# Layer 0 of a two-layer decoder: attention outputs and five output weights split once, stored as two parts, and loaded by GpSimd's queue

## Chip, cores and metric

The kernel runs on one core of one Trainium2 chip. The metric is the device time of one execution in microseconds; the time of a kernel is the median of several runs. The engines are PE (matrix products), DVE and ACT (elementwise work), POOL (GpSimd) and SP, which does nothing here but issue transfers. PE's granted clock was 0.999 of full speed in the profiled execution of the kernel before, so the clock plays no part below.

## The reference, cut to what matters

Two layers over a sequence of 1024 positions and 1024 features, all in float32. Layer 0 is differential attention with 8 head pairs, layer 1 forgetting attention; after each come a residual sum with layer norm, a gated feed-forward block with a short convolution, and another layer norm. The change touches layer 0's attention alone:

```python
q, k, v = jnp.split(x @ w_qkv, 3, axis=-1)        # rotary on q and k
p = masked_softmax(s * scale, causal_mask(...))   # two score maps per head pair
a = p[:, :, 0] - lam * p[:, :, 1]
o = rms_norm(jnp.einsum('bhqk,bhkd->bqhd', a, v), subln_g) * (1.0 - lambda_init)
y = o @ w_o                                       # the output projection
h = layer_norm(alpha * h + y, ln1_g, ln1_b)
```

In the kernel the output of pair p is one tile of 128 features by 1024 positions, and the output projection is a sum over the 8 pairs: `y = sum over p of o_p^T @ w_o[p]`, with `w_o[p]` a slab of 128 x 1024.

## The kernel before

**Two parts for each operand.** A float32 product is made of three products of a reduced format: an operand x is split into `h`, the rounded value, and `l = x - h`, and PE adds up `h·h + h·l + l·h` (`mm3`, lines 104 to 110). A split (`split`, lines 93 and 95) is one copy on ACT, which writes `h`, and one subtraction on DVE, which reads x and `h` and writes `l`. Every operand of every projection passes through it once.

**Layer 0, pair by pair.** While the scores, softmax and values of pair p run, PE's spare places are filled with the steps of a second job, one product with a whole slab column block at a time: for p < 7 the projections q, k and v of pair p + 1 (48 steps), for p = 7 the output projection's first part (`out_first`, 64 steps). `pulse` counts these steps, and `after(n, f)` calls f when n more steps have been issued. The instructions thus stand in one written order; a planner of the framework then lays the order of each engine, with a time model of its own: it starts, in the written order's priority, what its model has ready, and gives a tile its place in memory when an earlier tile's last reader is done. On the chip each engine and each issuing queue then works strictly in the order laid. `high_priority` moves a few instructions forward.

**The way of an output.** The values of a pair are made in two groups of four query blocks. When a group is done, `diff_values` copies the result from PE's memory into the pair's tile `of` (line 624), squares it, lets PE sum the squares over features (lines 639 and 640), and scales it by the norm (lines 642 to 647, the last instruction being that of line 647 on DVE). There is one buffer for `of`. After the second group `Values.finish` stores the whole tile, 512 KB, to `od[p]` in memory (line 1625). Since the values lag behind, pair p's store falls in pair p + 1's stretch, and the next user of the buffer is pair p + 1's first copy of line 624. For the output projection `fetch_o` (line 866) loads `od[k]` again and `load_o` splits it into four tiles of 128 x 512, taken from the same 16 + 16 places (`xh`, `xl`) that hold the layer's input while the projections run.

**The output weights.** `ahead(i)` loads slab i raw into one of two `wst` buffers, which the softmax uses too, and `ready(i)` splits it into `wh` and `wl` (three buffers each). Slabs 24 to 31 are the eight of `w_o`. Slab 27 goes into four half tiles (`ready_halves`).

**Queues.** SP issues nearly all transfers: loads, stores, and per pair some 50 small ones for the rotation of q and k and for laying their parts into place. POOL casts one operand of each score product (`qz`, line 548), with two buffers for each of the two heads, and issues a few transfers at the very beginning.

**The beginning.** `first_pair_rotary` runs q and k of pair 0 for both halves of the sequence, rotates them through transfers, runs v, and then the loop over pairs begins. The pool `probT` (tiles `pt`, three buffers) is not used before the first values; the tiles `q1` (seven) are not used before pair 1's projections are done.

Of the kernel before, what the change touches and what calls it, by code (L numbers as in the profile page):

```python
# [9 lines left out]
F32 = mybir.dt.float32  # L10
F32R = mybir.dt.float32r
# [8 lines left out]
P = 128  # L20
# [3 lines left out]
NP = 8  # L24
# [31 lines left out]
W_V, FRAC = 1, 0  # L56
TURN0 = 9
TT1 = 3


class Trunk:
# [319 lines left out]
    def first_pair_rotary(self, t):  # L381


        dst = [self.tmp() for s in range(3)]
        self.xh, self.xl = {}, {}
        pos = self.rope_angles()
        self.nc.scalar.preload_act_table_set("trig_and_small")
        self.warm()
        self.first_loads(pos)
        self.consts()  # L390
        r = {}
        for c in range(2):
            ps = [self.mbank() for _ in range(2)]
            for _ in zip(*[self.dense_steps(ps[s], *self.w[s], c, FILL * (c + s == 0)) for s in range(2)]):
                pass
            if c:
                self.turn(dst, r, 0)
            for s in range(2):
                self.result(0, s, c, ps[s], dst[s], t)
            if c == 0:  # L400
                self.exp_table()
            self.gather(dst, r, c, self.nc.gpsimd)
            if c:
                self.halves(dst, t, 0)
        self.lam()
        for c in range(2):
            self.ready(3) if c else self.ahead(3)
            ps = self.mbank()
            self.dense(ps, *self.w[2], c)
            self.result(0, 2, c, ps, dst[2], t)  # L410
            if c == 0:
                self.turn(dst, r, 1)
                self.halves(dst, t, 1)
            self.after(2 + 2 * c, self.turn_v, 0, c, dst[2], *t[5:7], True)
        self.ahead(4)

    def first_pair(self, l, t):

# [328 lines left out]
    def attention(self, l):  # L747
# [1 line left out]


        nc = self.nc
        self.od = self.dr.tile([NP, P, 1024], F32, name=f"od{l}")
        tiles = lambda p: [self.qtile((p + l) % 2) for _ in range(7)] + (
            [self.lp.tile([P, 1024], F32R, tag="lg", name=self.nm("kl"))] if l else [])
        self.slabs = [self.i[f"w{l}"][s * NP + p] for p in range(NP) for s in range(3)]
# [11 lines left out]
        for p in range(NP):  # L767
# [21 lines left out]
            for job in jobs:  # L789
                live, values = self.tick(live, values, job)  # L790
                w = job[0] + 1 + W_C - (W_V * self.coming(values) if l == 0 else 0)
# [66 lines left out]
    def accumulate(self, acc, ps, alpha):  # L858
        if alpha is None:
            self.nc.vector.tensor_tensor(acc, ps, acc, op=ALU.add)  # L860
        else:
            self.nc.vector.scalar_tensor_tensor(acc, acc, alpha, ps, op0=ALU.mult, op1=ALU.add)

    def fetch_o(self, l, k):
        t = self.lp.tile([P, 1024], F32, tag="lg", name=self.nm("og")) if l == 0 and k < 2 else self.tmp()
        self.nc.sync.dma_start(t, self.od[k])
        self.og[k] = t

    def load_o(self, k, src=None, cs=(0, 1)):
# [28 lines left out]
    def out_ahead(self, l, c):  # L898

        if c == 0:  # L900
            self.oh, self.ol, self.og = {}, {}, {}
            self.fetch_o(l, 0)
            self.after(8, self.load_o, 0, None, (0,))
        else:
            self.ahead(25)
            self.after(3, self.load_o, 0, None, (1,))
            self.after(4, self.fetch_o, l, 1)
            self.after(6, self.ready, 25)
            self.after(8, self.load_o, 1)
# [30 lines left out]
                del self.w[24 + k]  # L940
        self.ready(29)

    def ready_halves(self, i):

        st, self.w[i] = self.stage.pop(i), ([], [])
        for n in range(2):
            for t, which in zip(self.w[i], ("xh", "xl")):
                t.append(self.xtile(which))
            self.split(self.w[i][0][n], self.w[i][1][n], st[:, n * 512:n * 512 + 512])

    def out_first(self):


        self.ahead(26)
        for tt, n in enumerate((0, 0, 0, 0, 0, 16, 22, 28)):
            if n:
                self.after(n, self.acc_tile, tt)
            else:
                self.acc_tile(tt)
        for k, n in ((2, 2), (3, 5), (4, 36), (5, 42), (6, 56)):  # L960
            self.after(n, self.fetch_o, 0, k)
            self.after(n + 4, self.load_o, k)
        self.after(5, self.ready, 26)
        self.after(5, self.ahead, 27)
        self.after(10, self.ready_halves, 27)
        parts = [(tt, (0, 1)) for tt in range(TT1)] + [(tt, (0, 1, 2, 3)) for tt in range(TT1, 8)] + \
            [(tt, (2, 3)) for tt in range(TT1)]
        for i, (tt, ks) in enumerate(parts):
            if i == 8:
                del self.w[24], self.w[25]  # L970
                self.ready(28)
                self.ahead(29)
                self.after(5, self.ready, 29)
                self.after(5, self.ahead, 30)
            elif i == 7:
                self.ahead(28)
            for n in range(2):
                ps = self.mbank()
                for k in ks:
                    self.out_mm(ps, k, tt, n, ks[0], ks[-1])  # L980
                    yield
                self.after(1, self.accumulate, tt, n, ps, ALPHA if ks[0] == 0 else 1.0)
        del self.w[26], self.w[27]
# [575 lines left out]
class Values:  # L1559
# [61 lines left out]
    def finish(self):  # L1621
        if self.end is not None and next(self.end, True):
            self.over = True
            if self.last and self.p < NP - 1:
                self.k.nc.sync.dma_start(self.k.od[self.p], self.k.ofs.pop(self.p))


class Ffn:
# [176 lines left out]
```

## Time and profile before

| | |
|---|---|
| median of 3 runs | 2410.02 us (2407.67 to 2410.25) |
| profiled execution | 2409.52 us, of which 2407.7 us span from first to last instruction |
| PE busy | 2386.8 us, 99% of the span |
| DVE, ACT, POOL busy | 1916.2 us (80%), 1271.1 us (53%), 198.0 us (8%) |
| transferred | 312.25 MB, 130 GB/s on average |
| pair 0's first scores | at 49.6 us |
| the projection of pair 7 ends, the output projection begins | about 418 us |

A line of the profile names the source line, the engine, the operation, then output and inputs by the names of the tiles in the program (`m<-xh,wh`), the shape, and the count; then the busy time, the mean of one in nanoseconds, and the idle time of the engine just before, with what ended it. In a list by time the first two numbers are start and length, and square brackets give the idle time before. An engine with a small q (`SPq`) stands for its issuing queue. `m` and `s` are PE's result memory: four and two buffers.

### The profile page before, as it was taken

How to read it: one execution, taken by the hardware profiler on the slowest of the kernel's cores; microseconds unless marked ns; L12 is line 12 of the kernel's file. 1: busy time of each engine (PE TensorE's matmuls, PEld its weight loads, DVE VectorE, ACT ScalarE, POOL GpSimd, SP SyncE). 2: the span in 40 equal slices, each digit the busy share in tenths (PEclk: the TensorE clock that was granted, in tenths of full speed). 3: DMA queues.
4: the chain of work that ended last, by engine and by line, in shares of the span. 5: the costliest groups of instructions: out<-in, count | busy, mean ns of one | idle time of the engine just before them, and what ended most of it. 6: DMA issues, size and time to landing. Idle time of an engine off the chain costs nothing.

```text
span 2407.7 us, 33873 instructions
## 1 busy us (share of the span) xinstructions
PE 2386.8 (99%) x11691; PEld 1985.8 (82%) x11691; DVE 1916.2 (80%) x3748; ACT 1271.1 (53%) x2405; POOL 198.0 (8%) x396
## 2 busy tenths in 40 slices
PE   9999999999999999999999999999999999999998
PEld 7888887778888888888878888888888888888887
DVE  5888888889987876777767777778899887777768
ACT  4656666556544445444545555555465444445434
POOL 2111111010000110100100000000010001110000
PEclk9999999999999999999999999999999999999999
DMA  6223333521433557876332222224224335559662
GB/s 185 67 78 96 89 86 103 189 95 62 171 119 119 123 134 204 261 227 212 112 82 68 66 67 67 66 95 141 92 79 142 122 118 132 132 142 316 194 232 103
DMA packets 140331, 312.25 MB, mean 130 GB/s; under 512 B 20816, under 2 KB 27984, under 8 KB 140160
## 3 DMA queue, kind: packets, MB, share of 16 engines
q1 hardware_dynamic: 128960, 289.05, 36.9%
q0 software_dynamic: 10912, 20.98, 5.3%
q8 instruction: 92, 1.51, 0.3%
q14 instruction: 79, 0.65, 0.1%
q10 hardware_dynamic: 288, 0.07, 0.0%
HBM read 194.21 MB, written 82.25 MB: 115 GB/s over the span
## 4 chain that ended last, share of the span: by engine, by line
PE 85%; DVE 7%; DMA 3%; ACT 3%; issue 2%; SPq 1%; DVEq 0%; ACTq 0%
PE m L104 19%; PE m L110 19%; PE m L109 19%; PE s L104 5%; PE s L110 5%; PE s L109 5%; PE m L1587 4%; PE s L556 2%; PE s L557 2%; PE m L1614 2%; PE m L1613 1%; DVE xl L95 1%; DVE wo L95 1%; DVE s L564 1%; DMA wb<-in_wd 0%
## 5 line engine op out<-in xcount | busy, mean ns | idle before, releaser
L104 PE MATMUL m<-xh,wh 128*128 128x512 f32 x768 | 314.7, 410 | 1.3 <-DVE pt L95 0.7
L110 PE MATMUL m<-xh,wl 128*128 128x512 f32 x768 | 302.6, 394 | 0.0
L109 PE MATMUL m<-xl,wh 128*128 128x512 f32 x768 | 301.6, 393 | 0.0
L104 PE MATMUL m<-xh,wo 128*128 128x512 f32 x656 | 255.7, 390 | 0.0
L109 PE MATMUL m<-xl,wo 128*128 128x512 f32 x656 | 255.6, 390 | 0.0
L110 PE MATMUL m<-xh,wo 128*128 128x512 f32 x656 | 255.3, 389 | 0.0
L564 DVE CUSTOM_DVE_ANT_0 s<-s,mask 128x384 f32<-128x384 f32 (+7 forms) x256 | 194.2, 760 | 28.0 <-PE s L557 27.2
L93 ACT ACTIVATE wo<-wg 128x512 fp32r<-128x512 f32 (+1 forms) x168 | 102.2, 610 | 169.2 <-PE m L110 141.8
L93 ACT ACTIVATE pt<-m 128x512 fp32r<-128x512 f32 (+3 forms) x285 | 131.1, 490 | 102.5 <-PE m L1587 97.3
L95 DVE TENSOR_TENSOR pt<-m,pt 128x512 fp32r<-128x512 f32 (+3 forms) x285 | 152.7, 557 | 32.6 <-ACT pt L93 30.7
L110 PEld LDWEIGHTS m<-xh,wl 128*128 128x128 f32 x768 | 144.2, 188 | 31.6 <-DVE wl L95 0.7
L104 PEld LDWEIGHTS m<-xh,wh 128*128 128x128 f32 x768 | 144.6, 188 | 27.6 <-DVE pt L95 3.8
L109 PEld LDWEIGHTS m<-xl,wh 128*128 128x128 f32 x768 | 145.0, 189 | 22.8
L548 POOL CAST qz<-q 64x128 fp32r<-64x128 f32 x256 | 94.1, 369 | 819.8 <-PE s L557 726.2
L93 ACT ACTIVATE wo<-t 128x512 fp32r<-128x512 f32 x132 | 83.4, 632 | 127.0 <-PE m L110 81.4
L110 PEld LDWEIGHTS m<-xh,wo 128*128 128x128 f32 x656 | 123.1, 188 | 25.8
L104 PEld LDWEIGHTS m<-xh,wo 128*128 128x128 f32 x656 | 123.3, 188 | 24.7 <-ACT p L1280 0.2
L109 PEld LDWEIGHTS m<-xl,wo 128*128 128x128 f32 x656 | 123.3, 188 | 24.3
L95 DVE TENSOR_TENSOR wo<-wg,wo 128x512 fp32r<-128x512 f32 (+1 forms) x168 | 110.5, 659 | 33.0 <-ACT wo L93 32.3
L556 PE MATMUL s<-q,q 128*128 128x512 f32 (+4 forms) x384 | 133.7, 350 | 1.5 <-ACT wst L602 1.3
L95 DVE TENSOR_TENSOR wo<-t,wo 128x512 fp32r<-128x512 f32 x132 | 90.7, 688 | 49.1 <-ACT wo L93 48.8
L104 PE MATMUL m<-q,wo 128*128 128x512 f32 x328 | 128.6, 392 | 0.0
(386 smaller groups left out, 6328.3 us busy)
## 6 DMA issues: line engine op xcount, KB each, us to landing
wb<-in_wd SPq DMA_DIRECT2D x142, 256.0 KB, 5.4
wst<-in_w SPq DMA_DIRECT2D x46, 512.0 KB, 4.6
t<-in_wi SPq DMA_DIRECT2D x44, 512.0 KB, 5.3
ha<-ad SPq DMA_DIRECT2D x86, 256.0 KB, 4.8
wg<-in_wi SPq DMA_DIRECT2D x42, 512.0 KB, 4.3
ad<-t SPq DMA_DIRECT2D x40, 512.0 KB, 4.1
ha<-sd SPq DMA_DIRECT2D x66, 256.0 KB, 4.3
q<-q SPq DMA_DIRECT2D x128, 128.0 KB, 2.2
```

Source lines behind the costliest of these rows:

```text
L93: self.high = nc.scalar.activation(hi, src, AF.Copy, scale=1.0 if scale is None else scale)
L95: self.low = nc.vector.tensor_tensor(lo, src, hi.bitcast(F32), op=ALU.subtract)
L104: last = mm(out, wh, xh, start=start, stop=False)
L109: mm(out, wh, xl, start=False, stop=False)
L110: mm(out, wl, xh, start=False, stop=stop)
L548: nc.gpsimd.tensor_copy(qz[r:r + 64, :], q[r:r + 64, qt * P:qt * P + P])
L556: nc.tensor.matmul(sb[:, ks], q[:, qt * P:qt * P + P], kd[:, ks], start=True, stop=False)
L557: nc.tensor.matmul(sb[:, ks], qz[:m], kl[:m, ks], start=False, stop=True)
L564: self.nc.vector.tensor_tensor_reduce(sb[:, :ln], sb[:, :ln], self.mask[:, 1024 - ln:], 1.0, BIG, ALU.add, ALU.min, mn)
L1587: nc.tensor.transpose(tb[:, w:w + P], self.pts[q - self.q0][:, kt * P:kt * P + P], k.ident)
L1613: mm(o, self.v[0][:, vs], h, start=first, stop=False)
L1614: mm(o, self.v[0][:, vs], l, start=False, stop=last)
```

## The change

Layer 0 alone changes. The new lines:

- Two steps (`D_PK`) after a group's norm has been written out, `park` splits that half of `of`: `h` goes into a half tile of pool `bcast`, `l` is written over the half of `of` itself. Three steps (`D_PS`) later SP stores both, 256 KB each, to `od[0][p]` and `od[1][p]`. The single store of the whole tile is gone in layer 0.
- At the beginning `park_loads` loads slabs 25 to 29 into `pt` tiles (three, then two), and `park_weights` splits them, `h` into `q1` tiles and `l` in place. `h` is stored to `wd[0]` by ACT's queue, `l` to `wd[1]` by POOL's queue. `lam` and the loads of slabs 3 and 4 are written further ahead.
- In the output projection nothing of pairs 0 to 6 nor of slabs 25 to 29 is split any more. `get_half` loads the two parts of half an output (two transfers of 256 KB), `get_weight` those of a slab (two of 512 KB, or four of 256 KB for slab 27), all on POOL's queue. Slabs 24, 30 and 31 and the output of pair 7 are split as before.
- Three of the residual tiles (`acc_tile`) are loaded 1, 5 and 9 steps into `out_first`, not at its start.

```diff
+D_PK, D_PS, PK0 = 2, 3, 25
...
             self.gather(dst, r, c, self.nc.gpsimd)
+            if c == 0:
+                self.lam()
+                self.ahead(3)
+                self.ahead(4)
+                st = self.park_loads(25, 26, 27)
             if c:
                 self.halves(dst, t, 0)
-        self.lam()
+        self.wd = [self.dr.tile([5, P, 1024], F32, name=f"wd{j}") for j in range(2)]
+        self.park_weights(*st)
         for c in range(2):
-            self.ready(3) if c else self.ahead(3)
+            if c:
+                self.ready(3)
...
                 self.halves(dst, t, 1)
+                self.park_weights(*self.park_loads(28, 29))
             self.after(2 + 2 * c, self.turn_v, 0, c, dst[2], *t[5:7], True)
-        self.ahead(4)
...
+    def park(self, k, of, c):
+        cs = slice(c * 512, c * 512 + 512)
+        h = self.lp.tile([P, 1024], F32R, tag="lg", name=self.nm("ph"))[:, :512]
+        l = of[:, cs].bitcast(F32R)
+        self.split(h, l, of[:, cs])
+        for d, t in zip(self.od, (h, l)):
+            self.after(D_PS, self.nc.sync.dma_start, d[k][:, cs], t.bitcast(F32))
+
+    def park_loads(self, *which):
+        st = []
+        for i in which:
+            st.append((i, self.tt.tile([P, 1024], F32, tag="pt", name=self.nm("wo"))))
+            self.nc.sync.dma_start(st[-1][1], self.slabs[i])
+        return st
+
+    def park_weights(self, *st):
+        for i, t in st:
+            h, l = self.spare(F32R), t.bitcast(F32R)
+            self.split(h, l, t)
+            self.nc.scalar.dma_start(self.wd[0][i - PK0], h.bitcast(F32))
+            self.nc.gpsimd.dma_start(self.wd[1][i - PK0], l.bitcast(F32))
+
+    def get(self, dst, src):
+        for t, d in zip(dst, src):
+            self.nc.gpsimd.dma_start(t.bitcast(F32), d)
+
+    def get_o(self, n, *ks):
+        for i, (k, c) in enumerate((k, c) for k in ks for c in range(2)):
+            self.after(n + 2 * i, self.get_half, k, c)
+
+    def get_half(self, k, c):
+        self.oh[k, c], self.ol[k, c] = self.xtile("xh"), self.xtile("xl")
+        self.get((self.oh[k, c], self.ol[k, c]), [d[k][:, c * 512:c * 512 + 512] for d in self.od])
...
         if c == 0:
             self.oh, self.ol, self.og = {}, {}, {}
+        if l == 0:
+            if c == 0:
+                self.get_o(3, 0, 1)
+            else:
+                self.after(2, self.get_weight, 25)
+                self.get_o(4, 2)
+        elif c == 0:
             self.fetch_o(l, 0)
...
-        self.ahead(26)
-        for tt, n in enumerate((0, 0, 0, 0, 0, 16, 22, 28)):
+        self.get_weight(26)
+        for tt, n in enumerate((0, 0, 1, 5, 9, 16, 22, 28)):
...
-        for k, n in ((2, 2), (3, 5), (4, 36), (5, 42), (6, 56)):
-            self.after(n, self.fetch_o, 0, k)
-            self.after(n + 4, self.load_o, k)
-        self.after(5, self.ready, 26)
-        self.after(5, self.ahead, 27)
-        self.after(10, self.ready_halves, 27)
+        self.get_o(2, 3)
+        self.after(3, self.get_weight, 27, 0)
+        self.after(5, self.get_weight, 27, 1)
+        self.get_o(34, 4, 5)
+        self.get_o(52, 6)
...
             if i == 8:
                 del self.w[24], self.w[25]
-                self.ready(28)
-                self.ahead(29)
-                self.after(5, self.ready, 29)
+                self.get_weight(28)
+                self.after(5, self.get_weight, 29)
                 self.after(5, self.ahead, 30)
-            elif i == 7:
-                self.ahead(28)
...
     def finish(self):
         if self.end is not None and next(self.end, True):
             self.over = True
+            if self.l == 0 and self.p < NP - 1:
+                self.k.after(D_PK, self.k.park, self.p, self.k.ofs[self.p], self.q0 // 4)
             if self.last and self.p < NP - 1:
-                self.k.nc.sync.dma_start(self.k.od[self.p], self.k.ofs.pop(self.p))
+                of = self.k.ofs.pop(self.p)
+                if self.l:
+                    self.k.nc.sync.dma_start(self.k.od[0][self.p], of)
```

More of the change, by code (lines that the diff above doesn't have):

```diff
@@ L751, in attention @@
         nc = self.nc
-        self.od = self.dr.tile([NP, P, 1024], F32, name=f"od{l}")
+        self.od = [self.dr.tile([NP, P, 1024], F32, name=f"od{l}{j}") for j in range(2 - l)]
         tiles = lambda p: [self.qtile((p + l) % 2) for _ in range(7)] + (
@@ L862, in accumulate, with get_weight @@
             self.nc.vector.scalar_tensor_tensor(acc, acc, alpha, ps, op0=ALU.mult, op1=ALU.add)
+    def park(self, k, of, c):
[26 more added lines that the diff above has]
+        self.get((self.oh[k, c], self.ol[k, c]), [d[k][:, c * 512:c * 512 + 512] for d in self.od])
+    def get_weight(self, i, n=None):
+        src = [d[i - PK0] for d in self.wd]
+        if n is None:
+            self.w[i] = [self.wp.tile([P, 1024], F32R, tag=t, name=self.nm(t)) for t in ("wh", "wl")]
+            return self.get(self.w[i], src)
+        w = self.w.setdefault(i, ([], []))
+        for t, which in zip(w, ("xh", "xl")):
+            t.append(self.xtile(which))
+        self.get([t[n] for t in w], [d[:, n * 512:n * 512 + 512] for d in src])
     def fetch_o(self, l, k):
-        t = self.lp.tile([P, 1024], F32, tag="lg", name=self.nm("og")) if l == 0 and k < 2 else self.tmp()
-        self.nc.sync.dma_start(t, self.od[k])
+        t = self.tmp()
+        self.nc.sync.dma_start(t, self.od[0][k])
         self.og[k] = t
@@ L941, in out_early @@
         self.ready(29)
[L943 to L949, printed above, removed]
     def out_first(self):
-        self.ahead(26)
-        for tt, n in enumerate((0, 0, 0, 0, 0, 16, 22, 28)):
+        self.get_weight(26)
+        for tt, n in enumerate((0, 0, 1, 5, 9, 16, 22, 28)):
             if n:
```

## The prediction, written before the change was run

> **What bounds the kernel now.** I read the first page for the share of each engine, then the engines' busy time by stretches, then the waits of PE, then the single stalls in order of time.
>
> ```profile
> span 2407.7 us, 33873 instructions
> PE 2386.8 (99%) x11691; PEld 1985.8 (82%) x11691; DVE 1916.2 (80%) x3748; ACT 1271.1 (53%) x2405; POOL 198.0 (8%) x396
> ```
>
> PE is the bound nearly everywhere: 2407.7 - 2386.8 = 20.9 us of the span are idle on it. The change touches no matmul, so all that it can give back lies in those 20.9 us, and only in those of layer 0's attention, which ends near 530 us. By stretches (columns: window and its length, then busy us and count on PE, PEld, DVE, ACT, POOL, then clock, DMA share, GB/s):
>
> ```profile
> 8.00:66.00 58.00, 57.62 (x265) 47.30 (x263) 35.48 (x94) 28.71 (x59) 14.41 (x32) 1.00 0.55 166
> 344.00:398.00 54.00, 53.51 (x272) 44.31 (x271) 44.11 (x106) 33.11 (x71) 5.09 (x16) 1.00 0.29 82
> 410.00:443.00 33.00, 29.18 (x141) 22.32 (x140) 28.95 (x63) 21.44 (x44) 2.56 (x8) 1.00 0.67 214
> ```
>
> The opening (8 to 66 us) and one pair's stretch (344 to 398) leave PE idle for 0.4 to 0.5 us. The change of work from pair 7's projection to the output projection (410 to 443) leaves 33.00 - 29.18 = 3.8 us, with DVE busy for 28.95 of 33. The stalls there and a little later, each with its length and what ended it:
>
> ```profile
> 413.29 0.66 PE L524 MATMUL m<-ident,t 128*128 128x128 f32 x4 [0.89 <-ACT t L479]
> 420.35 0.50 PE L104 MATMUL m<-wh,xh 128*128 128x512 f32 x1 [0.25 <-ACT xh L93]
> 425.44 0.66 PE L1587 MATMUL m<-ident,p 128*128 128x128 f32 x4 [1.81 <-DVE acc L889]
> 440.82 0.50 PE L104 MATMUL m<-xh,xh 128*128 128x512 f32 x1 [0.82 <-ACT xh L93]
> 487.49 0.50 PE L104 MATMUL m<-wh,xh 128*128 128x512 f32 x1 [0.81 <-DVE acc L889]
> ```
>
> Two more follow when the values of pair 7 and the norm are done; the waits of PE from 410 to 530 name them (total us, times, longest):
>
> ```profile
> PE m L104 <- ACT pt L93: 0.7, 1, 0.7
> PE m L1050 <- DVE acc L1732: 0.3, 1, 0.3
> ```
>
> Together 0.89 + 0.25 + 1.81 + 0.82 + 0.81 + 0.7 + 0.3 = 5.6 us. That is the most this change can win.
>
> **Part 1, what leaves the output projection.** From 404 to 490 us ACT and DVE split the fetched outputs (tiles og and t) and the weights (wst):
>
> ```profile
> L93 ACT ACTIVATE xh<-t 128x512 fp32r<-128x512 f32 x10 | 5.8, 623 | 2.8 <-DMA t<-od 2.7
> L93 ACT ACTIVATE wh<-wst 128x1024 fp32r<-128x1024 f32 x5 | 5.3, 1062 | 6.1 <-DMA wst<-in_wo 4.5 <-PE m L110 1.6
> L95 DVE TENSOR_TENSOR xl<-t,xh 128x512 fp32r<-128x512 f32 x10 | 6.6, 686 | 1.2 <-ACT xh L93 1.2
> L95 DVE TENSOR_TENSOR wl<-wst,wh 128x1024 fp32r<-128x1024 f32 x5 | 6.1, 1220 | 1.4 <-ACT wh L93 1.4
> L95 DVE TENSOR_TENSOR xl<-og,xh 128x512 fp32r<-128x512 f32 x4 | 2.7, 706 | 0.0
> ```
>
> Of the five wide weight splits, weight 24's stays and four go; weight 27 is split in two halves, like an output. So 10 + 4 + 2 = 16 half splits and 4 wide ones leave: DVE 16 x 0.69 + 4 x 1.22 = 15.9 us, ACT 16 x 0.62 + 4 x 1.06 = 14.2 us. Nothing of it counts by itself; it counts where PE waited for those engines.
> - 425.44: an accumulation came late on a DVE that was behind with its work. Ahead of it the wide split of weight 25 (1.22) and two half splits (1.38) go, 2.6 us against a stall of 1.81: all of it.
> - 420.35 and 440.82: PE waited for such a split itself (outputs of pair 1; outputs of pair 3 and weight 27). All of 0.25 and 0.82, if the loads land in time (below).
> - 487.49: again a late accumulation. Two wide splits and two half ones go ahead of it, 3.8 us against 0.81: all of it.
> - 413.29: the copy of a projection's result was late on ACT, behind an exponential that itself waited for DVE. One half split (0.69) goes ahead of that; I take half, 0.45, with bounds 0 and 0.89.
> - The two at the end lie behind PE and ACT work that stays: I take half of the 0.7, 0.35, and nothing of the 0.3, with bounds 0 and 1.0.
> Gain: 1.81 + 0.25 + 0.82 + 0.81 + 0.45 + 0.35 = 4.5 us.
>
> **Part 2, the splits behind the norms.** Fourteen halves get an ACT copy of 0.62 and a DVE subtraction of 0.69 (rows above), and a pair gets four stores on SP in place of one. Per pair that is 1.4 us more on a DVE that is busy for 44.11 of 54 us, and 1.2 on ACT with 33.11: room, but the place is tight. The output tile `of` has one buffer, and the next pair's first result (L624) can be copied into it only when the store has landed:
>
> ```profile
> 349.74 0.69 DVE L647 SCALAR_TENSOR_TENSOR of<-m,of 128x512 f32<-128x512 f32 x1
> 351.20 0.34 SPq L1625 DMA_DIRECT2D od<-of  x1
> 351.20 3.20 DMA od<-of
> 354.50 0.58 ACT L624 COPY of<-m 128x512 f32<-128x512 f32 x1 [3.48 <-DMA od<-of]
> 354.98 1.12 ACT L602 ACTIVATE p<-s,nm 128x1024 f32<-128x1024 f32 x1
>   DMA od<-of: 8.3, 3
> 366.97 0.39 PE L556 MATMUL s<-q,q 128*128 128x256 f32 x1 [0.49 <-ACT wst L602]
> ```
>
> The norm ends at 350.43, the store lands at 354.4, and ACT has stood idle for 3.48 us for it (over the kernel 8.3 us in 3 places, the row without a time). Behind it hangs a chain that ends in the 0.49 us at 366.97. Now the split stands between: 0.62 + 0.69 and some 0.7 of waiting make `of` free about 2.0 us later, as `l` is written into `of` and stored from there. The two counts of steps (2 and 3) cost less, since they are counted from the norm's matmul, some 5 us ahead of its last instruction. L602, which waits behind L624 on ACT, then PE 12 us later, would be late by as much. Bounds for the six changes from pair to pair: 0, if the order of ACT's work is laid so that L602 goes ahead, to 6 x 2.0 = 12 us. No gain is possible here, as nothing is taken away. The order on an engine is laid by a planner that starts what is ready by its own account, and the copy of 0.62 fits into the 3.48 us of idle ACT; so I am near the lower end, 0.25 us each: 1.5 us. SP's extra issues are 3 x 0.34 = 1.0 us a pair; what stands behind them are gathers that PE does not wait for.
>
> **Part 3, five weights at the start.** 5 x 1.06 = 5.3 us on ACT, 5 x 1.22 = 6.1 on DVE, five issues on ACT's queue and five on POOL's, 2.5 MB read and 5 MB written. The row 8 to 66 has 29.3 us of idle ACT and 22.5 of idle DVE. Scores have a reserve: their data are there at 41.6, PE takes them at 49.63.
>
> ```profile
> 41.36 0.53 POOL L548 CAST qz<-q 64x128 fp32r<-64x128 f32 x2 [2.01 <-DMA q<-q]
> 49.63 0.22 PE L556 MATMUL s<-q,q 128*128 128x128 f32 x1
> ```
>
> The 7.5 MB share the DMA engines with the small transfers of the rotation between those two rows, so part of these 8 us goes. Bounds 0 and 3 us (three round trips in a row, each 1 us longer); I take 0.5, nearer to the cover of 8 us.
>
> **Part 4, the loads on POOL's queue.** 28 loads of outputs and 10 of weights from about 404 to 478 us.
>
> ```profile
> L1330 POOL DMA_DIRECT2D ad<-t x4 | 2.2, 562 | 84.1 <-DVE t L1327 29.9 <-PE s L110 27.4 <-DVE t L1328 26.8
> POOL qz L548 <- PE s L557: 55.6, 15, 12.7
> ha<-ad POOLq DMA_DIRECT2D x2, 256.0 KB, 5.8
> ad<-t POOLq DMA_DIRECT2D x4, 512.0 KB, 7.4
> 10.00:20.00 10.00, 10.00 (x45) 8.05 (x44) 9.27 (x22) 8.33 (x18) 2.33 (x4) 1.00 1.05 377
> 400.00:410.00 10.00, 9.77 (x47) 7.86 (x46) 8.00 (x17) 7.09 (x13) 1.17 (x2) 1.00 0.77 219
> 410.00:420.00 10.00, 9.11 (x45) 7.23 (x43) 8.65 (x18) 7.46 (x13) 0.66 (x3) 1.00 0.57 181
> 420.00:430.00 10.00, 7.89 (x39) 5.79 (x39) 10.00 (x18) 6.12 (x11) 0.46 (x1) 1.00 0.75 200
> 430.00:440.00 10.00, 9.99 (x51) 7.70 (x49) 7.70 (x24) 5.35 (x15) 1.16 (x4) 1.00 0.81 305
> ```
>
> An issue takes 0.56 us: 38 x 0.56 = 21 us of POOL in 74. Queued behind a load that waits for a free tile are the casts of the scores' operand. In this stretch (400 to 480) POOL waits for PE 15 times, 55.6 us in all, because it casts as soon as the buffer is read, four scores ahead; a load may block it for several us before PE notices. Landing takes 5.8 to 7.4 us. The last weight for the step at 440.82 is asked for by about 425 and lands by 433. I cost this at nothing; bounds 0 and 3 us, if the bytes pile up.
>
> **The sum**, against the profiled execution's 2409.5 us (1.8 of it outside the span; it stands 0.5 below the median of 2410.0): 2409.5 - 4.5 + 1.5 + 0.5 = **2407.0 us**, 0.12% under the median. A measurement of this kernel can tell about 0.2%, 4.8 us, from no change.
>
> **Rivals.**
> 1. *All stalls go, the splits hide.* 2409.5 - 5.6 = 2403.9 us, faster by 0.25%. For it: the idle ACT ahead of L624. Against: DVE has no gap of that kind.
> 2. *The late `of` decides: slower.* If L624 stays ahead of L602 on ACT, each of six pairs loses 2.0 us: 2409.5 - 4.5 + 12 + 0.5 = 2417.5. For it: the 0.49 us that hang on this chain today, so no reserve is left. Against: an order that puts L602 first. It turns the sign once a pair loses 0.7 us (4.0 / 6).
> 3. *The loads pile up.* Outputs and weights are twice as many bytes: from 400 to 440 us 2 MB more of outputs 0 to 3 and 1.5 MB of weights 25 to 27, on top of (219 + 181 + 200 + 305) GB/s x 10 us = 9.1 MB. At 305 GB/s (row above) 12.5 MB take 41 us, at 377 GB/s 33: just about all of the stretch. Accumulations and the step at 440.82 would then wait as now, and 1.81 + 0.82 stay: 2407.0 + 2.6 = 2409.6, no change. The Trainium skill, page "DMA: Bandwidth & Descriptors", section "Issuing engines are not separate DMA queues", says that transfers from SP, ACT and GpSimd end up on the same 16 engines and that another issuer saves the issuing time alone. By that rule POOL's queue gives no bandwidth of its own and this rival holds; were the queues independent, SP's transfers would land as before and only POOL's 7.4 us would count. The trace fits the rule as far as it goes: at a DMA share of 1.05 all transfers together made 377 GB/s.
> 4. *A queued load blocks the casts* is too short for a case of its own: it costs up to 2 us, within the range.
>
> **Numbers.** Forecast (2405 to 2409.5) 0.38, rival 1 0.25, rival 2 with lesser forms of it 0.25, rival 3 0.12. Faster by over 0.2% (under 2405.2): rival 1 and a little of the forecast, 0.28. Slower by over 0.2% (over 2414.8): rival 2 without its lesser forms, 0.20, and 0.03 of rival 3 with the start's bound at its bad end: 0.23. Within: 0.49. The range goes from 2402 (all bounds good, and 2 us of spread between runs) to rival 2's 2417.
>
> **What would show it.** Right: the five stalls from 410 to 490 shrink to under 1 us together; DVE's busy time from 410 to 443 falls by some 8 us (9 half and 2 wide splits of those that leave lie there); the wait of L624 for stores of `of` does not end in longer stalls of scores 12 us later; POOL's loads land before 440. Wrong: PE idle over 1 us in a stretch of a pair (rival 2), scores late at 49.63 (part 3), or out matmuls that wait for DMA at 420 to 445 (rival 3).

## The result, and the profile after

The changed kernel takes 2429.85 us (median of 6 runs, 2427.41 to 2430.99), the kernel before 2409.97 us beside it (6 runs, 2407.67 to 2411.06): 1.0083 times as long, with a 95% interval of 1.0070 to 1.0096. It is slower by 19.9 us, and outside the predicted range. Line numbers of the new file are higher by 1 to 8 up to the scores (L93 became L94, L104 L105, L556 L564, L624 L632) and by some 50 for the values' transposes (L1587 became L1638).

The first page of the changed kernel, then stretches by the columns named in the prediction: the opening, one pair, the change to the output projection with the same 141 matmuls as 410 to 443 before, and two short stretches.

```profile
PE 2392.0 (99%) x11691; PEld 1989.7 (82%) x11691; DVE 1918.5 (79%) x3747; ACT 1269.8 (52%) x2404; POOL 230.7 (10%) x441
```

```profile
8.00:66.00 58.00, 50.44 (x222) 40.45 (x220) 31.16 (x72) 27.82 (x51) 15.37 (x31) 0.97 0.81 268
50.00:60.00 10.00, 3.99 (x13) 2.77 (x13) 2.27 (x5) 3.04 (x5) 1.14 (x2) 0.83 0.58 154
358.00:412.00 54.00, 53.00 (x269) 44.00 (x268) 44.56 (x108) 33.85 (x72) 8.04 (x16) 1.00 0.32 92
424.30:463.70 39.40, 31.57 (x141) 24.17 (x140) 26.31 (x65) 16.53 (x37) 17.04 (x35) 0.91 1.01 343
435.00:445.00 10.00, 5.52 (x20) 3.54 (x21) 6.42 (x13) 4.79 (x10) 5.45 (x11) 0.79 1.03 385
```

The span is 2427.6 us, so PE is idle for 2427.6 - 2392.0 = 35.6 us instead of 20.9. The opening had 0.4 us of idle PE and has 7.6; the ten microseconds from 50 to 60 have 6.0. The change to the output projection takes 39.4 us for what took 33.0, at a DMA share of 1.01 where it was 0.67. The pair's stretch has 1.0 us of idle PE where it had 0.5. In both stretches of 10 us the granted clock lies under 1.

Both kernels run the same 11,691 matmuls. So the start of the n-th matmul in one trace minus its start in the trace of before is the delay at that point. Taken at the matmuls that before starts at 85, 405, 480 and 2390 us, the delay of the profiled executions splits into four stages (of one execution each, so differences of a microsecond between two kernels say little):

| stage, by the time of before | delay gained, us |
|---|---|
| opening, to 85 | 9.5 |
| pairs, 85 to 405 | 4.8 |
| handover to the output projection, 405 to 480 | 6.4 |
| the rest, 480 to 2390 | -1.1 |
| sum | 19.6 |

**The opening.** SP's queue, before and after: the same small transfers of the rotated q and k.

```profile
40.34 1.19 SPq L309 DMA_DIRECT2D q<-q  x2
41.62 0.55 SPq L291 DMA_DIRECT2D q<-t  x1
42.26 1.18 SPq L518 DMA_DIRECT2D t<-t  x2
43.53 0.54 SPq L309 DMA_DIRECT2D q<-q  x1
```

```profile
42.11 3.33 SPq L310 DMA_DIRECT2D q<-q  x2
45.54 2.07 SPq L292 DMA_DIRECT2D q<-t  x1
47.71 2.69 SPq L526 DMA_DIRECT2D t<-t  x2
51.54 0.50 SPq L310 DMA_DIRECT2D q<-q  x1
```

Five issues that took 2.9 us take 8.1, and the transfer behind them, for which the first score waits, is issued 8.0 us later. What fills the engines meanwhile are the stores of the split weights; these two rows are those issued from 37 to 52 us, with their size and the median time to landing. Below them are waits of ACT and PE's waits for scores.

```profile
wd<-sp ACTq DMA_DIRECT2D x3, 512.0 KB, 6.8
wd<-wo POOLq DMA_DIRECT2D x3, 512.0 KB, 6.9
```

```profile
52.49 0.63 ACT L94 ACTIVATE q<-t 128x512 fp32r<-128x512 f32 x1 [7.38 <-DMA t<-t]
58.30 1.06 ACT L94 ACTIVATE sp<-wo 128x1024 fp32r<-128x1024 f32 x1 [3.04 <-DMA wo<-in_wo]
59.76 0.37 ACT L610 ACTIVATE wh<-s,nm 128x128 f32<-128x128 f32 x1 [0.40 <-ACT sp L94]
53.88 0.30 PE L564 MATMUL s<-q,q 128*128 128x128 f32 x1 [3.92 <-DMA q<-q]
60.27 0.39 PE L564 MATMUL s<-q,q 128*128 128x256 f32 x1 [2.40 <-ACT wh L610]
66.58 0.44 PE L564 MATMUL s<-q,q 128*128 128x384 f32 x1 [1.82 <-ACT wst L610]
```

PE waits 3.92 + 2.40 + 1.82 = 8.1 us for the first score maps. Only the first of these is a wait for a small transfer. The other two are waits for exponentials, in front of which ACT has the split of a parked weight (`sp<-wo`); it stood 3.04 us, and before the third wait 2.10 us, until that weight's raw load had landed. SP issued the first of these loads late as well, at 53.46 (at 48.06 in a run below without the stores). Part of the rest of the 9.5 us is the clock, which the row 50 to 60 gives as 0.83.

**The handover.** In the kernel before, the store of the output tile and the copy that needs its place:

```profile
406.73 0.33 SPq L1625 DMA_DIRECT2D od<-of  x1
410.41 0.59 ACT L624 COPY of<-m 128x512 f32<-128x512 f32 x1 [1.03 <-PE m L110]
```

After: GpSimd's queue (the first and last of eight loads), SP's store of the output tile, ACT, DVE, and all of PE's stalls from 427 to 448 us:

```profile
417.66 0.56 POOL L899 DMA_DIRECT2D xl<-od  x1 [3.94 <-PE m L111]
...
421.91 0.55 POOL L899 DMA_DIRECT2D xh<-od  x1
```

```profile
423.21 0.44 SPq L338 DMA_DIRECT2D od<-of  x1
431.86 0.59 ACT L632 COPY of<-m 128x512 f32<-128x512 f32 x1 [4.68 <-DMA od<-of]
432.58 0.54 DVE L521 TENSOR_TENSOR t<-t,rope 128x256 f32<-128x256 f32 x1 [7.13 <-DMA t<-t]
```

```profile
427.24 0.66 PE L532 MATMUL m<-ident,t 128*128 128x128 f32 x4 [0.58 <-ACT t L487]
434.17 0.50 PE L647 MATMUL m<-hl,ones 128*128 128x512 f32 x1 [1.77 <-ACT hl L94]
436.03 0.50 PE L648 MATMUL m<-hl,ones 128*128 128x512 f32 x1 [1.36 <-DVE hl L96]
438.47 0.33 PE L564 MATMUL s<-q,q 128*128 128x128 f32 x1 [0.55 <-ACT wst L610]
440.18 0.33 PE L1638 MATMUL m<-ident,p 128*128 128x128 f32 x1 [0.93 <-DVE p L620]
442.48 0.80 PE L105 MATMUL m<-wh,xh 128*128 128x512 f32 x1 [1.97 <-ACT t L487]
447.69 0.66 PE L1638 MATMUL m<-ident,p 128*128 128x128 f32 x4 [0.35 <-DVE acc L945]
```

PE waits for no load of an output or a weight. But the eight loads issued from 417.66 to 421.91 (seven of 256 KB and one of 512, 2.4 MB) are in the engines when SP stores the 256 KB of `of`. That store lands 431.8 - 423.2 = 8.6 us later. Before, 512 KB took 3.20 us in a pair's stretch, and at this place under 3.7, since the copy at 410.41 waited for PE alone. Now ACT stands for 4.68 us in front of the copy L632, DVE for 7.13 us because the rotation's transfers of 16 and 32 KB are late as well. The stalls of the splits are gone: the accumulation's 1.81 is 0.35, the 0.25 and 0.82 for split operands and the 0.81 do not appear. New waits for norm, softmax and copies stand in their place.

**The pairs.** PE's waits from 85 to 400 us before and to 405 after:

```profile
PE s L556 <- ACT wst L602: 1.3, 3, 0.5
PE m L104 <- DVE pt L95: 0.5, 2, 0.3
PE m L1587 <- DVE p L612: 0.2, 1, 0.2
```

```profile
PE s L564 <- ACT wst L610: 2.6, 5, 0.6
PE m L1638 <- DVE p L620: 2.0, 4, 0.8
PE m L532 <- ACT t L487: 0.6, 1, 0.6
PE s L564 <- ACT p L610: 0.5, 1, 0.5
PE m L105 <- DVE pt L96: 0.4, 1, 0.4
```

From 2.0 us to 6.1: PE waits for the softmax on ACT and DVE, in many small pieces. In all of this stretch L632 waits for PE alone; no wait for a store of `of` is left there. But ACT's order has changed. In five pairs the split of a rotated operand, which waits 1.65 to 2.77 us for its transfer, now stands in front of the softmax's exponential, here in one of them:

```profile
263.94 0.63 ACT L94 ACTIVATE q<-t 128x512 fp32r<-128x512 f32 x1 [2.77 <-DMA t<-t]
264.48 1.10 ACT L610 ACTIVATE wst<-s,nm 128x1024 f32<-128x1024 f32 x1
```

The wait of 0.82 us for `p`, the longest of its row, follows at 267.52. Before has no such place.

### The profile page after: what moved, and what is told of

It reads as the page before. It is cut to its first block, busy times and chain, and to the rows that moved or that the text cites. A ratio compares the mean times of both kernels' runs of the same rounds, so it can differ in the third digit from the quotient of the medians.

```text
span 2427.6 us, 33968 instructions
## 1 busy us (share of the span) xinstructions
PE 2392.0 (99%) x11691; PEld 1989.7 (82%) x11691; DVE 1918.5 (79%) x3747; ACT 1269.8 (52%) x2404; POOL 230.7 (10%) x441
## 4 chain that ended last, share of the span: by engine, by line
PE 83%; DVE 6%; DMA 4%; ACT 3%; issue 2%; SPq 2%; DVEq 0%; ACTq 0%
PE m L105 18%; PE m L111 18%; PE m L110 18%; PE s L105 5%; PE s L111 5%; PE s L110 5%; PE m L1638 4%; PE s L564 2%; PE s L565 2%; DMA t<-t 2%; PE m L1665 2%; PE m L1664 1%; DVE xl L96 1%; ACT p L610 1%; SPq L526 1%
## 5 line engine op out<-in xcount | busy, mean ns | idle before, releaser
L105 PE MATMUL m<-xh,wh 128*128 128x512 f32 x768 | 315.3, 411 | 0.4 <-DVE pt L96 0.4
L105 PE MATMUL m<-xh,wo 128*128 128x512 f32 x656 | 255.7, 390 | 0.0
L94 ACT ACTIVATE pt<-m 128x512 fp32r<-128x512 f32 (+3 forms) x285 | 131.4, 491 | 117.7 <-PE m L1638 112.4
L94 ACT ACTIVATE wo<-wg 128x512 fp32r<-128x512 f32 (+1 forms) x168 | 102.2, 609 | 169.9 <-PE m L111 142.1
L96 DVE TENSOR_TENSOR pt<-m,pt 128x512 fp32r<-128x512 f32 (+3 forms) x285 | 152.7, 556 | 33.1 <-ACT pt L94 31.1
L556 POOL CAST qz<-q 64x128 fp32r<-64x128 f32 x256 | 102.2, 400 | 782.6 <-PE s L565 691.2
L105 PEld LDWEIGHTS m<-xh,wh 128*128 128x128 f32 x768 | 145.2, 189 | 26.1 <-DVE pt L96 3.1
L94 ACT ACTIVATE wo<-t 128x512 fp32r<-128x512 f32 x132 | 83.5, 632 | 125.6 <-PE m L111 80.8
L564 PE MATMUL s<-q,q 128*128 128x512 f32 (+4 forms) x384 | 134.6, 353 | 12.1 <-ACT wst L610 5.3
L105 PEld LDWEIGHTS m<-xh,wo 128*128 128x128 f32 x656 | 123.3, 188 | 24.7
L96 DVE TENSOR_TENSOR wo<-wg,wo 128x512 fp32r<-128x512 f32 (+1 forms) x168 | 110.5, 659 | 34.0 <-ACT wo L94 33.3
L96 DVE TENSOR_TENSOR wo<-t,wo 128x512 fp32r<-128x512 f32 x132 | 90.7, 688 | 49.5 <-ACT wo L94 49.3
L105 PE MATMUL m<-q,wo 128*128 128x512 f32 x328 | 128.6, 392 | 0.0
```

Source lines behind the costliest of these rows:

```text
L94: self.high = nc.scalar.activation(hi, src, AF.Copy, scale=1.0 if scale is None else scale)
L96: self.low = nc.vector.tensor_tensor(lo, src, hi.bitcast(F32), op=ALU.subtract)
L105: last = mm(out, wh, xh, start=start, stop=False)
L556: nc.gpsimd.tensor_copy(qz[r:r + 64, :], q[r:r + 64, qt * P:qt * P + P])
L564: nc.tensor.matmul(sb[:, ks], q[:, qt * P:qt * P + P], kd[:, ks], start=True, stop=False)
```

## The experiments

Each was timed beside the kernel before; the ratio is to that, with its 95% interval. The four columns at the right are delays of the profiled executions by stage, worked out as above.

| run | median us | ratio | opening | pairs | handover | rest |
|---|---|---|---|---|---|---|
| the change | 2429.85 | 1.0083 (1.0070 to 1.0096) | 9.5 | 4.8 | 6.4 | -1.1 |
| e1_no_start | 2419.45 | 1.0045 (1.0033 to 1.0058) | 0.2 | 4.4 | 6.2 | -1.6 |
| e2_own_half | 2430.5 | 1.0097 (1.0083 to 1.0111) | 10.7 | 2.9 | 5.7 | 1.1 |
| e3_outputs_only | 2419.88 | 1.0048 (1.0036 to 1.0061) | -0.1 | 4.6 | 5.7 | 1.0 |
| e4_weights_only | 2427.42 | 1.0076 (1.0062 to 1.0090) | 8.9 | 0.0 | 8.9 | 1.9 |
| e5_sp_queue | 2432.75 | 1.0098 (1.0082 to 1.0113) | 11.7 | 5.5 | 7.5 | -0.8 |
| e6_no_stores | 2420.32 | 1.0054 (1.0042 to 1.0067) | 3.6 | 3.4 | 6.6 | 0.6 |
| e7_quarter | 2428.79 | 1.0082 (1.0069 to 1.0096) | 10.5 | 3.8 | 4.7 | 0.8 |
| e8_one_store | 2421.77 | 1.0055 (1.0043 to 1.0068) | -0.6 | 2.8 | 7.1 | 1.7 |
| e9_held | 2427.68 | 1.0082 (1.0068 to 1.0096) | 9.8 | 5.6 | 2.3 | -0.9 |
| e10_paced | 2419.88 | 1.0047 (1.0035 to 1.0060) | 1.1 | 1.8 | 5.2 | 2.0 |
| e11_two_holds | 2420.09 | 1.0047 (1.0033 to 1.0061) | 0.3 | 2.6 | 1.8 | 4.5 |
| e12_two_outputs | 2415.96 | 1.0029 (1.0017 to 1.0040) | 0.2 | 1.3 | 5.2 | 2.1 |

Theory A says that the opening is lost to the weights' stores, D that the handover is lost to the loads' bytes, which make small transfers and the store of `of` late.

### The opening: nothing done there, and all but the stores

```diff
-                st = self.park_loads(25, 26, 27)
-        self.park_weights(*st)
-                self.park_weights(*self.park_loads(28, 29))
...
-        src = [d[i - PK0] for d in self.wd]
+        src = [d[0] for d in self.wd]
...
+            if l == 0 and p == 2 and n == 1:
+                for d, w in zip(self.wd, self.w[i + s]):
+                    self.nc.sync.dma_start(d[0], w.bitcast(F32))
```

The last lines store one split projection weight during pair 1's stretch; it is what all twelve weight loads read later.

> Nothing is split or stored for the output weights at the beginning; the ten weight loads of the output projection read one pair of stored tiles over and over (left out: the five weights' own splits and stores, so the output projection uses a wrong weight), with the same bytes on the same queue. Theory A (the stores at 37 to 52 us fill the DMA engines and the small transfers in front of pair 0's scores come late, 10.2 us of PE): the 10 us come back and nothing else moves, 2419.5 us, 2418 to 2421.5. Rival B (the beginning's delay would be made up or caused again later, for example because the later stages wait for something else): 2425 to 2430.

2419.45 us, as theory A has it. PE has no idle time from 50 to 60 us again, and the other stages keep their delays:

```profile
50.00:60.00 10.00, 10.00 (x49) 8.37 (x47) 6.94 (x29) 4.34 (x14) 2.07 (x7) 1.00 0.26 63
```

The second run keeps loads, splits and the moved places, and leaves out the stores alone:

```diff
-            self.nc.scalar.dma_start(self.wd[0][i - PK0], h.bitcast(F32))
-            self.nc.gpsimd.dma_start(self.wd[1][i - PK0], l.bitcast(F32))
```

> The beginning as in the changed kernel, with its loads, its five splits and its earlier places of other work, but without the ten stores; one pair of tiles is stored later and loaded in place of each weight (left out: the five weights' own values). Theory A (the stores' bytes delay the small transfers): 10 us come back, 2419.5 us, 2418.5 to 2421. Rival E (the splits on ACT and DVE stand ahead of the rotation's work): 2425 to 2430. Rival F (the loads and the earlier places): 2425 to 2430 as well, told from E by the trace.

2420.32 us: 9.5 us come back by leaving out the ten stores alone. The profiled execution, 2423.81 us, was one of the two longer of five (2420.05 to 2425.31) and shows 3.6 us in the opening. In it PE waits 2.72 us at 54.33 behind the split of a parked weight, for whose raw load ACT has stood 2.90 us, which is rival E's mechanism. So the splits are not free in every execution, but without the stores three of five lose no more than a microsecond against the run with nothing done at the beginning. SP's issues of 128 KB from 42 to 47 us take 0.49 to 0.59 us again. A holds for the stores; what they make late are the small transfers and also the raw loads of the last two weights.

### One part at a time

> Outputs are split behind their norms and loaded as two parts by the GpSimd queue; all weights as before, raw, split in the output projection. Theory A (start) and D (bytes pile up): 10 us of the start are gone, of 7.0 MB of loads between 417 and 450 us 2 MB less, 2415 us, 2411 to 2418; the pairs' 4 us stay. Rival B: 2425 to 2430. If the splits behind the norms cost nothing but the start and the weights' loads do, it is 2408 to 2411.

Here the beginning and the five weights are as before (`ahead`, `ready`, `ready_halves` at their old places). 2419.88 us: neither the 2415 expected nor the better case. With 2 MB less to load, the handover still loses 5.7 us of 6.4.

> Five weights are split at the beginning and loaded as two parts; all outputs as before, stored whole and split in the output projection. Theory A: the 10 us of the start are there, the pairs cost nothing, the handover at 410 to 450 us is at about its old cost: 2420 us, 2418 to 2423. If the loads of the weights by themselves pile up at the handover, 2424 to 2428. Rival B (the start is not what costs): 2408 to 2413.

Here `park` is out, and outputs are stored whole, fetched and split as before. 2427.42 us, in the range given to a pile-up of the weights' loads alone. Outputs alone cost 11.4 us over before, weights alone 18.9, both together 19.9: at the handover the two parts do not add, so the loss does not grow with the bytes in proportion. Either set of loads is enough for 6 to 9 us (5.7 and 8.9). With weights alone, the waits that end last are again for transfers:

```profile
420.74 1.15 ACT L94 ACTIVATE xh<-og 128x512 fp32r<-128x512 f32 x2 [4.57 <-DMA og<-od]
447.63 0.47 ACT L610 ACTIVATE t<-s,nm 128x256 f32<-128x256 f32 x1 [6.93 <-DMA q<-t]
```

And the pairs: 4.6 us with outputs alone, 0.0 with weights alone. They belong to the splits behind the norms and their stores.

### Who waits for the store of `of`

```diff
-        h = self.lp.tile([P, 1024], F32R, tag="lg", name=self.nm("ph"))[:, :512]
-        l = of[:, cs].bitcast(F32R)
+        hl = self.lp.tile([P, 1024], F32R, tag="lg", name=self.nm("ph"))
+        h, l = hl[:, :512], hl[:, 512:]
```

> The low part of an output goes into the unused half of the tile that holds the high part, not over the output itself, so the output tile is free when the subtraction has read it and no longer when its store has landed. Theory C (what is lost behind the beginning is the wait of the next pair's first copy for the store of the output tile: 4.68 us of idle ACT at 431.86, a smaller one in each pair): the 4 us of the pairs and most of the 6 us at 425 to 450 come back, 2429.9 - 8 = 2422 us, 2419 to 2424. Rival D (the transfers pile up at 417 to 450 and the rotation's small ones are late in any case): the pairs' part at most, 2425 to 2429.

2430.5 us: theory C falls. ACT at the handover shows why:

```profile
422.52 0.59 ACT L632 COPY of<-m 128x512 f32<-128x512 f32 x1 [1.13 <-PE m L111]
...
431.02 0.63 ACT L94 ACTIVATE hl<-sq 128x512 fp32r<-128x512 f32 x1 [4.52 <-DMA od<-ph]
```

The copy no longer waits; a few instructions later ACT waits as long for the same late store, since the next norm's tile `hl` takes the place of the stored one. At the handover, which tile is held is not the point, the landing is. In the pairs it is: the exponential is no longer behind a rotated operand in any of them, the waits for `p` fell from 2.0 to 0.2 us, and the pairs' delay went from 4.8 to 2.9 us. At the place shown above:

```profile
263.02 1.12 ACT L610 ACTIVATE wst<-s,nm 128x1024 f32<-128x1024 f32 x1 [2.26 <-DVE nm L572]
```

The other runs agree: the seven kernels that write `l` over the output all have the five places and lose 3.4 to 5.6 us in the pairs; the four that give all outputs a half of their own have none and lose 1.8 to 2.9.

```diff
-        for d, t in zip(self.od, (h, l)):
-            self.after(D_PS, self.nc.sync.dma_start, d[k][:, cs], t.bitcast(F32))
+        self.after(D_PS, self.nc.sync.dma_start, self.od[c][k], hl.bitcast(F32))
```

This run goes on from outputs alone, with the own half and one store for both parts.

> Outputs alone, weights as before; the low part goes beside the high part in one tile, and one store of 512 KB takes both, two stores a pair instead of four. Against the run with outputs alone (2419.9 us, 4.7 us of it in the pairs from 85 to 405 us): if SP's extra issues cost what the own half left (2.4 us), the pairs lose under 1 us, 2416 us, 2414.5 to 2417.5; if the splits' own work on DVE and ACT costs it, the pairs keep 2 to 3 us, 2417.5 to 2419.

2421.77 us, over the range of both cases. In the pairs 2.8 us stay, as the second case had it: SP's extra issues cost nothing that shows. The rest hangs on the splits' work on ACT and DVE or on the doubled bytes of the stores; these were not told apart, nor was it found which engine and which place in its order. The handover got worse, 7.1 us.

### Whose queue, and how many bytes

```diff
-            self.nc.gpsimd.dma_start(t.bitcast(F32), d)
+            self.nc.sync.dma_start(t.bitcast(F32), d)
```

> All 38 loads of the output projection go through SP's queue, in their written places between the rotation's small transfers. Theory Q (GpSimd's own queue lets the large loads run ahead of the small transfers and of the store of the output tile): at 405 to 450 us 3 to 6 of the 6.4 us come back, 2424 to 2427 us. Rival D (the bytes themselves fill the engines, whoever issues them, and some small transfers still stand behind large ones): 2428 to 2434.

2432.75 us, handover 7.5, as rival D had it. Another queue changes nothing for the better. The Trainium skill, page "DMA: Bandwidth & Descriptors", section "Issuing engines are not separate DMA queues", has it so, and this run agrees with its 7.5 us against 6.4.

```diff
     def get_half(self, k, c):
+        if 1 <= k < 4:
+            self.oh[k, c], self.ol[k, c] = self.oh[0, c], self.ol[0, c]
+            return
```

> In the output projection outputs 1 to 3 are replaced by output 0 and weights 26 and 27 by weight 25 (left out: their loads, so that the sum is over the wrong operands); matmuls and the rest as in the changed kernel. 2.0 MB of loads instead of 7.0 from 417 to 450 us. Theory D (the loads fill the engines and the small transfers and the store of the output tile land late): the 6.4 us of 405 to 450 come back, 2423.5 us, 2421.5 to 2425; the stalls that the splits caused before are gone as well, so up to 4 us more, 2419. Rival G (the wait of GpSimd's queue for free tiles holds up the casts, or the missing staging of the loads): 2427 to 2430.

2428.79 us, which rival G had. But it does not tell the theories apart: with tiles free, the planner moved the loads of outputs 4 to 6 and of two weights up, and from 417 to 434 us it loads 12 x 256 and 4 x 512 KB, 5.2 MB, where the change loads 14 x 256 and 3 x 512 KB, 5.2 MB. The next run holds those loads behind a copy on POOL that reads a residual tile.

```diff
+    def gate(self, tt):
+        self.held = self.nc.gpsimd.tensor_copy(self.small(1, "gt"), self.acc[tt][:, :1]).ins
...
-        self.get_o(34, 4, 5)
+        self.after(34, self.gate, 4)
+        self.get_o(35, 4, 5)
```

> As the run with a quarter of the loads (outputs 1 to 3 replaced by output 0, weights 26 and 27 by weight 25: the sum is over the wrong operands), whose later loads had moved up into the places of those left out; here they are held until the fifth residual tile has been added up, so that only 2 MB are loaded from 417 to about 440 us. Theory D (the loads' bytes make the store of the output tile and the rotation's small transfers land late): the store lands in 4 to 5 us, not 8.8, and the 6.4 us of 405 to 450 come back, 2423.5 us, 2420 to 2425. Rival G (not the bytes but the order of the engines' work): 2427.5 to 2430.

```profile
430.43 0.59 ACT L632 COPY of<-m 128x512 f32<-128x512 f32 x1 [2.12 <-DMA od<-of]
```

ACT's wait is 2.12 us instead of 4.68, DVE's 4.10 instead of 7.13. The store lands in 6.5 us instead of 8.6, though not in the 4 to 5 expected. From 405 to 460 us the delay changes by -0.4 us, where the run before it, which lacks the hold alone, gained 4.7: D holds at its place. The total, 2427.68 us, does not show it (it lies in G's range), because the held loads then cost 2.7 us from 460 to 480, and opening and pairs came out 1.1 us higher in this execution.

### Loads spread out

Outputs alone, with the low part in its own half, and outputs 0 to 3 loaded in the order of their use:

```diff
-                self.get_o(3, 0, 1)
+                self.after(3, self.get_half, 0, 0)
+                self.after(5, self.get_half, 1, 0)
...
+        for n, tt, kc in ((4, 0, ((2, 0), (3, 0))), (12, 2, ((0, 1), (1, 1), (2, 1), (3, 1)))):
+            self.after(n, self.gate, tt)
+            for k, c in kc:
+                self.after(n + 1, self.get_half, k, c)
```

> Outputs alone (weights raw as before), low part beside the high part in its own tile, and the loads of outputs 0 to 3 in the order of their use, in three groups of 1.0, 1.0 and 2.0 MB, the second and third held until the first and the third residual tile have been added up. Same bytes as in the run with outputs alone (2419.9 us). Theory D: 2 us less in the pairs and 3 to 5 of 5.7 us less at the handover, 2414 us, 2412 to 2416. Rival G: the pairs' 2 us alone, 2417 to 2419.5; if PE then waits for the later groups, 2418 to 2422.

2419.88 us, no better than outputs alone. By stages both parts of theory D are there: 1.8 us in the pairs, and the delay falls from 2.9 us at 405 to 0.7 at 430 us of before. That is the gain that the prediction had counted on, 2.2 us of it. Then it is lost again. The 4.4 us by 455 hold a wait of 2.30 us for an accumulation, behind a DVE and an ACT that stood until the raw load of a weight (`wst`) had landed, ACT for 3.21 us. The 3.0 us more by 480 come where a residual tile, asked for at 461.32 between the held loads, is late:

```profile
468.88 0.69 DVE L942 SCALAR_TENSOR_TENSOR acc<-acc,m 128x512 f32<-128x512 f32 x1 [3.61 <-DMA acc<-in_x]
```

> As the paced run (2419.9 us) without the third hold, which had put the loads of outputs 4 and 5 beside that of the last residual tile at 461 us (accumulation late by 3.6 us). Theory D: PE's loss at 460 to 480 us (3.0 us) goes, 2417 us, 2415.5 to 2418.5. Rival (the loss moves on to another place again): 2419 to 2421.

The last hold is taken out. From 460 to 480 us the delay is 0.0 now, the handover 1.8 in all. 2420.09 us all the same: 3.9 us appear from 480 to 500, ended by a wait for the values' split (`pt`, L96) of 3.16 us in one piece. The rival was right. In front of that wait ACT stands 6.68 us, until 492.46, for the raw load of another weight; why that load is late was not followed further.

```diff
-            if self.l == 0 and self.p < NP - 1:
+            if self.l == 0 and self.p < 2:
                 self.k.after(D_PK, self.k.park, self.p, self.k.ofs[self.p], self.q0 // 4)
```

> Only the outputs of pairs 0 and 1 are split behind their norms and loaded as two parts (1 + 1 MB at the handover); the outputs of pairs 2 to 6 and all weights as before. If the pairs' splits cost 0.4 us each and the handover's stalls of before (up to 4.5 us) fall by the share of the four half splits, it is within 2 us of before, 2407 to 2411 us. If also 2 MB of loads at this place make the store of the output tile and the small transfers late, 2412 to 2417.

2415.96 us, 7.4 over before: the second case. Eight loads of 256 KB, issued from 405.10 to 409.52, stand around the store of `of`:

```profile
405.10 0.58 POOL L892 DMA_DIRECT2D xl<-od  x1 [4.56 <-PE m L111]
408.26 0.33 SPq L1685 DMA_DIRECT2D od<-of  x1
415.15 0.58 ACT L625 COPY of<-m 128x512 f32<-128x512 f32 x1 [6.33 <-DMA od<-of]
417.38 0.66 PE L525 MATMUL m<-ident,t 128*128 128x128 f32 x4 [3.44 <-ACT t L480]
```

Two MB are enough, at a DMA share of 0.94 from 405 to 415 us where it was 0.60, and the whole chain is in view: loads, store, copy, PE. No version beat the kernel before.

## Why the prediction was wrong, point by point

**The sum.** The four terms were to give -4.5 + 1.5 + 0.5 + 0 = -2.5 us; the four stages gave 19.6.

**Part 1, -4.5 us for the stalls: right that they go, the gain shown only in part.** Of the four stalls from 420 to 490 us (3.69 us) the 0.35 at 447.69 is all that answers to them, the one at 413 has become 0.58. DVE's busy time over the same matmuls fell from 28.95 to 26.31 us, not by 8; the stretch is 6.4 us longer and holds other work. The gain shows only where the loads were paced: 2.2 us up to 430, where the forecast had 1.81 + 0.25 + 0.45 = 2.5 for the three stalls. In the changed kernel it is covered by what part 4 did.

**Part 2, 1.5 us for the pairs: size and mechanism off.** It cost 4.8 us. I let `of`, held "as `l` is written into `of` and stored from there", cost only the wait of L624 for the store, and relied on a planner that lays the order so that this wait is small. It did so: in the pairs L632 waits for PE alone. But the order that it laid has its own price, the exponential behind a rotated operand in five pairs, and with a half of its own for `l` some 2 us are gone. What is left, 1.8 to 2.9 us, comes with the added work and stores. I had covered them with "the copy of 0.62 fits into the 3.48 us of idle ACT" and with room on DVE; their mechanism stays open. Rival 2's store wait did come once, at the handover, with 4.68 us.

**Part 3, 0.5 us for the start: the step that failed most.** It cost 9.5 us. The failing sentences are "part of these 8 us goes" and the bound of 3 us, "three round trips in a row, each 1 us longer". I had the bytes (7.5 MB) and did not turn them into time. Six stores of 512 KB, 3.1 MB, issued from 37.6 to 44.8 us, take 3.1 MB / 377 GB/s = 8.3 us at the rate of the row 10 to 20 that I quoted. And the reserve was not 8 us: the cast at 41.36 is not the last thing that the first score needs. It also waits for a transfer that SP issued at 43.53; after the change the same transfer lands 2.2 us after its issue, so some 3.9 us were left of it before PE's start at 49.63 (an estimate from these rows). Issued 8.0 us later, it overran them by about 4.1 us, and the delay at the matmul that before starts at 50 us is 4.3 us. A small transfer behind the stores is late by the queue ahead of it, not by its own 1 us: an ACT that reads one waited 7.38 us. The second thing missed was the order on ACT. "29.3 us of idle ACT" covered the splits, but two of them stand in front of pair 0's exponentials and wait for their raw loads; PE's waits of 2.40 and 1.82 us lie behind them.

**Part 4, 0 us for the loads, bounds 0 and 3: wrong.** "The last weight ... lands by 433" was about the loads themselves, and PE indeed waits for none of them. I asked whether the loads are in time, and rival 3 whether the work of the projection would wait for them; neither asked what else was using the engines: the store of `of`, and the rotation of pair 7. Rival 3 computed the very figure, 12.5 MB in 33 to 41 us, "just about all of the stretch", and priced it as the loss of 2.6 us of gain. The handover lost 6.4 us. Over its 141 matmuls PE's idle time grew from 3.8 us to 7.8 (7.5 of it the seven rows), by 4.0. Its busy time grew from 29.2 to 31.6 us for the same matmuls; these 2.4 us fit the clock, 0.79 from 435 to 445 where it was 1.00. That share is worked out and was not tried by itself. So the clock does play a part after the change, unlike in the kernel before. The loads are 40 and not 38, as weight 27 takes four; nothing hangs on it.

**Rivals and range.** The rule cited for rival 3 held. Rival 2 named the right sign, with a store wait that came at one place alone. The range had been bounded by the reserve of one chain at a time; the common cause, large transfers in front of small ones, touched two of its four terms.

## What to carry to other kernels

A large transfer that nothing waits for is not free if small ones that something waits for share its time: sum up all bytes of a stretch, divide by the rate the trace shows at a full share, and compare with the reserve of the smallest transfer on a chain, not with the large one's own due time. Take that reserve from the last transfer that the chain needs, not from the first. Moving work out of a busy stretch pays only if what is put in its place, here twice the bytes at the moment when tiles come free, leaves the small transfers of that stretch their time; a share of 0.94 was already too much here. Staging raw data early and splitting late costs engine time and buys transfers that may come early; loading in final form can start only when the final place is free.

## What the runs showed of the hardware

SP's issue was slower while large stores of other queues were under way. Its issue of a 128 KB transfer took 0.54 to 0.59 us before (39 to 44 us) and 1.63 to 2.07 us at 42 to 47 us after, when ACT and GpSimd had six stores of 512 KB under way; without these stores it took 0.49 to 0.59 there. So the queue behind it is late twice, by its own issues and by the landings. A full DMA share alone did not do this: from 441 to 445 us after, at a share of 1.04, these issues took 0.50 to 0.59 us. Why the stores did is open.

An idle PE costs more than its idle time. After waits of 3.92 and of 1.77 + 1.36 us the granted clock of the ten microseconds around them was 0.83 and 0.79, so part of them ran at the lower of its two levels, 1.2 instead of 2.4 GHz; PE's busy time over the whole kernel rose from 2386.8 to 2392.0 us with the same matmuls.
